# Conv module's end in a conv/retention trunk: output weights' low halves behind the sums, idle full-width products, gate product first, rsqrt as one GpSimd power, smaller first loads

## The chip, the cores and the metric

The kernel runs on one core of a Trainium2 chip. The core has five engines that run side by side, each through its own list of instructions in order: TensorE (PE) for matrix products, VectorE (DVE) and ScalarE (ACT) for element-wise work, GpSimd (POOL) for slower element-wise work, and SyncE (SP), which only issues transfers (ACT issues some too). A semaphore wait holds back everything behind it on that engine. The metric is the device time of one execution in microseconds (us), as the median of several runs; one further execution is taken with a profiler, and all timelines here are from that one.

## The reference

One sequence of 512 tokens, 1024 channels, two layers in float32. Each layer is a mixer and a causal feed-forward block (FFN), each behind an RMS norm and added to the residual stream; at the end stands another RMS norm.

```python
def conv_module(x, w_in, dw_w, dw_b, ln_g, ln_b, w_out):     # mixer of layer 0
    h = x @ w_in                                             # 1024 -> 2048
    a, gate = jnp.split(h, 2, axis=-1)
    h = a * jax.nn.sigmoid(gate)
    h = causal_dwconv(h, dw_w, dw_b)                         # 31 taps per channel
    mu, var = mean(h), mean((h - mu)**2)                     # over the channels
    h = (h - mu) * rsqrt(var + EPS) * ln_g + ln_b
    return silu(h) @ w_out                                   # 1024 -> 1024

def conv_ffn(x, w_in, dw_w, dw_b, w_out):                    # both layers
    a, u = jnp.split(x @ w_in, 2, axis=-1)                   # 1024 -> 2 x 2816
    return (silu(causal_dwconv(a, dw_w, dw_b)) * u) @ w_out  # 3 taps

for i in range(2):
    x = x + mixer_i(rmsnorm(x))          # conv_module, then retention with 4 heads
    x = x + conv_ffn(rmsnorm(x))
return rmsnorm(x)
```

## The kernel before

Channels lie on the 128 partitions (eight groups of 128), tokens along the free axis, so a tile of one channel group is 128x512. Every product of float32 operands is made as three products of halves: each operand is split into a high half, a rounded copy made by ACT, and a low half, the rest, made by DVE. `mm3` (L237 to L239) and `mm3_all` (L244 to L248) issue high x high, low x high, high x low. Weights come in chunks of 1 MB into three buffers `wr`; ACT makes `wh` (L213) and DVE `wl` (L217). A chunk's buffer is free again when both have read it.

A scheduler with a timeline of its own orders each engine's instructions; `issue_after` adds a constraint to that order. The order inside the conv module is written out as a string of words (L44): `m` is the products of one channel group, a and gate, `t` its convolution by taps on ACT, POOL and DVE, `b` and `p` its convolution as products with a banded matrix on TensorE (groups 3, 4, 6, 7), `s` a common shift, `c` the centring of a group's result (L565) with its square (L575), `q` the column sums, `u` the layer norm's statistics and their broadcast, `v` scale, shift and silu to the operands `z`. The tokens are done in two halves, `a` and `b`. The output product `co` (L244 to L248) starts with half `a` while half `b` gets its statistics.

The steps that the change and the prediction touch are these.

- Ten of a group's 31 taps: ACT scales (L520, L523), POOL adds (`pla`, L524). The other 21 are DVE's (`tp`, L533), and DVE adds the two parts (`cs`, L535). Group 5 is the last to end (at 122.81 us).
- The sums of the layer norm: for groups 0 to 5, the centred values and squares are first added up in `lnad` and `lnaq` (L578, L579; groups 4 and 5 by DVE, others by POOL), and TensorE sums them over the partitions in columns (`lna`, `lnb`, L557). Groups 6 and 7 are summed by themselves. Group 7 comes in halves (`cs7a`, `cs7b` by way of `yb7a`, `cq7a` and so on, L499 to L505, with transfers in between).
- The statistics: small DVE operations on 128x2 (L625 to L628), `rsqrt_small` (L274 to L286, a shift and three Newton steps), two diagonal tiles `lnda` (L636), two broadcast products `lnba` (L638).
- `split_behind` says behind which instructions a chunk's low halves may be issued: chunks 8 and 9, the first of the output weights, have the last gate and the last tap sum (L674).
- In the FFN, `ffn_half` makes for each group of 128 the products `fa`, `fu`, the three taps, silu, and the product `fy` (L715). In the last half of the last FFN it also issues one transposition of the residual (`xq`, L941) per group, for a token-major final norm; behind each set of them stand the transfers `xt` on SP's queue.
- The norms' statistics (`Rstd`, L299 to L313): transposes, a reduction, `rsqrt_small`, a diagonal tile (`n0d` to `n3d`), a broadcast product (`n0b` to `n3b`).

## Time and profile before

| | us |
|---|---|
| median of the runs | 1329.04 |
| the profiled execution | 1330.59 |
| its span, first to last instruction | 1328.8 |
| PE busy | 1306.9 (98%) |
| DVE busy | 750.4 (56%) |
| ACT busy | 491.5 (37%) |
| POOL busy | 351.4 (26%) |
| mean granted TensorE clock | 0.989 |

A row of a timeline gives start, duration, engine, line, operation, the tile written and the tiles read with their shape, the count, and in brackets how long the engine sat idle before it and what ended that. Rows of equal kind that follow one another are joined, so a duration with a count above one is the whole of them. Matrix products are pipelined: the step from one to the next is shorter than the duration of one. The granted clock is the share of full speed that TensorE's throttle lets through.

### The profile page before, as it was taken

How to read it: one execution, taken by the hardware profiler on the slowest of the kernel's cores; microseconds unless marked ns; L12 is line 12 of the kernel's file. 1: busy time of each engine (PE TensorE's matmuls, PEld its weight loads, DVE VectorE, ACT ScalarE, POOL GpSimd, SP SyncE). 2: the span in 40 equal slices, each digit the busy share in tenths (PEclk: the TensorE clock that was granted, in tenths of full speed). 3: DMA queues.
4: the chain of work that ended last, by engine and by line, in shares of the span. 5: the costliest groups of instructions: out<-in, count | busy, mean ns of one | idle time of the engine just before them, and what ended most of it. 6: DMA issues, size and time to landing. Idle time of an engine off the chain costs nothing.

```text
span 1328.8 us, 15111 instructions
## 1 busy us (share of the span) xinstructions
PE 1306.9 (98%) x6004; PEld 1090.8 (82%) x6004; DVE 750.4 (56%) x1059; ACT 491.5 (37%) x647; POOL 351.4 (26%) x293
## 2 busy tenths in 40 slices
PE   9999799999999999999999999999999999999997
PEld 7888788888888888878888888888878888888886
DVE  6998667666335554563565644644766462255544
ACT  5545454434223433423333332332534341133332
POOL 1859131687206110220213203203211110011110
PEclk9999699999999999999999999999999999999999
DMA  7543232131322222322332422422143222223121
GB/s 289 215 155 103 72 104 95 66 125 66 125 95 95 95 79 86 137 96 103 91 116 76 130 97 82 159 72 92 67 139 111 95 97 97 103 84 120 55 79 64
DMA packets 39814, 140.49 MB, mean 106 GB/s; under 512 B 11840, under 2 KB 21824, under 8 KB 25536
## 3 DMA queue, kind: packets, MB, share of 16 engines
q1 hardware_dynamic: 36432, 135.15, 29.0%
q10 hardware_dynamic: 3312, 4.38, 1.0%
q8 instruction: 47, 0.77, 0.2%
q14 instruction: 23, 0.19, 0.0%
HBM read 130.07 MB, written 2.10 MB: 99 GB/s over the span
## 4 chain that ended last, share of the span: by engine, by line
PE 91%; DVE 4%; DMA 2%; POOL 1%; ACT 1%; issue 1%; SPq 0%; DVEq 0%; ACTq 0%
PE fu L238 6%; PE fu L237 6%; PE fu L239 6%; PE fa L238 6%; PE fa L237 6%; PE fa L239 6%; PE vg L237 4%; PE vg L238 4%; PE vg L239 4%; PE lo L238 3%; PE lo L239 3%; PE lo L237 3%; PE fo L237 3%; PE fo L238 3%; PE fo L239 3%; PE qk L237 2%
## 5 line engine op out<-in xcount | busy, mean ns | idle before, releaser
L217 DVE TENSOR_TENSOR wl<-wr,wh 128x1024 fp32r<-128x1024 f32 (+1 forms) x222 | 285.7, 1290 | 277.6 <-ACT wh L213 273.5
L213 ACT CAST wh<-wr 128x1024 fp32r<-128x1024 f32 (+1 forms) x222 | 231.4, 1045 | 409.4 <-PE fo L239 82.7
L706 POOL MEMSET ap<- 128x2 f32 x44 | 4.2, 99 | 398.6 <-DVE ft L711 338.6
L715 DVE TENSOR_TENSOR fy<-fu,ft 128x512 f32<-128x512 f32 x44 | 30.3, 689 | 66.6 <-PE fu L239 35.0
L840 POOL TENSOR_TENSOR gg<-gg,gn 128x512 f32<-128x512 f32 x16 | 23.9, 1495 | 153.1 <-ACT gg L839 153.1
L709 ACT ACTIVATE ft<-ap,prm 128x512 f32<-128x512 f32 x44 | 35.7, 814 | 69.4 <-DVE ap L707 69.4
L533 DVE SCALAR_TENSOR_TENSOR tp<-hp,prm,tp 128x512 f32<-128x512 f32 x80 | 55.5, 741 | 0.4
L524 POOL TENSOR_TENSOR pla<-pla,plt 128x512 f32<-128x512 f32 x36 | 49.9, 1387 | 8.3 <-ACT pla L520 4.9
L813 POOL TENSOR_TENSOR rs<-rs 128x512 f32<-128x512 f32 x16 | 26.7, 1687 | 85.8 <-DVE rs L812 81.5
L710 DVE SCALAR_TENSOR_TENSOR ft<-ap,prm,ft 128x512 f32<-128x512 f32 x44 | 35.8, 815 | 17.3 <-ACT ft L709 17.2
L712 ACT ACTIVATE ft<-ft 128x512 f32<-128x512 f32 x44 | 27.9, 633 | 44.8 <-DVE ft L711 44.3
L713 POOL TENSOR_TENSOR ft<-ft,n3r 128x512 f32<-128x512 f32 x22 | 32.3, 1467 | 29.0 <-ACT ft L712 29.0
L713 POOL TENSOR_TENSOR ft<-ft,n1r 128x512 f32<-128x512 f32 x22 | 31.6, 1435 | 28.3 <-ACT ft L712 28.3
L711 DVE SCALAR_TENSOR_TENSOR ft<-ap,prm,ft 128x512 f32<-128x512 f32 x44 | 37.1, 843 | 1.4
L397 DVE TENSOR_TENSOR xT<-ro,xT 128x512 f32<-128x512 f32 x32 | 22.0, 687 | 24.2 <-PE ro L239 24.1
L491 PE MATMUL cph<-ph,cmat 128*128 128x128 f32 x288 | 32.9, 275 | 1.2 <-DMA ph<-hq 1.2
L491 PEld LDWEIGHTS cph<-ph,cmat 128*128 128x128 f32 x288 | 32.7, 192 | 1.7 <-issue 1.4
L523 ACT ACTIVATE plt<-hp,prm 128x512 f32<-128x512 f32 x36 | 25.7, 722 | 18.3 <-POOL pla L524 18.1
L885 POOL TENSOR_TENSOR gg<-gg,on 128x512 f32<-128x512 f32 x16 | 20.2, 1295 | 33.5 <-ACT on L884 33.5
L707 DVE TENSOR_TENSOR ap<-fa,n3r 128x512 f32<-128x512 f32 x22 | 15.1, 691 | 24.6 <-PE fa L239 24.6
L707 DVE TENSOR_TENSOR ap<-fa,n1r 128x512 f32<-128x512 f32 x22 | 15.1, 690 | 17.0 <-PE fa L239 16.9
L751 POOL TENSOR_SCALAR near<-prod 128x512 f32<-128x512 f32 x11 | 23.5, 2136 | 0.9
(1563 smaller groups left out, 3841.0 us busy)
## 6 DMA issues: line engine op xcount, KB each, us to landing
wr<-in_weights_dram SPq DMA_DIRECT2D x107, 1024.0 KB, 4.8
cmat<-in_mats_dram SPq DMA_DIRECT2D x4, 2304.0 KB, 10.5
wr<-in_weights_dram SPq DMA_DIRECT2D x6, 512.0 KB, 3.8
yt<-yq SPq DMA_DIRECT2D x48, 64.0 KB, 2.1
xT<-in_xt_dram SPq DMA_DIRECT2D x4, 512.0 KB, 7.4
xt<-xq SPq DMA_DIRECT2D x32, 48.0 KB, 3.5
ph<-hq SPq DMA_DIRECT2D x16, 64.0 KB, 2.2
dm<-in_decay_dram ACTq DMA_DIRECT2D x4, 256.0 KB, 2.7
```

Of the source, the lines that this page charges most:

```text
L213: latest[0] = act.copy(hi[:, o:o + n], raw[:, s + o:s + o + n])
L217: latest[1] = dve.tensor_tensor(out=lo[:, o:o + n], in0=raw[:, s + o:s + o + n], in1=hi[:, o:o + n].bitcast(F32), op=ALU.subtract)
L237: pe.matmul(ps, wh, xh, start=first, stop=False)
L238: pe.matmul(ps, wl, xh, start=False, stop=False)
L239: pe.matmul(ps, wh, xl, start=False, stop=last)
L491: pe.matmul(ps[:, g * P:(g + 1) * P], mats[i][g][:, s, :], ph[:, g, NSH - 1 - s:NSH - 1 - s + P], start=s == 0, stop=s == NSH - 1)
L524: pool.tensor_tensor(out=pl, in0=pl, in1=tm, op=ALU.add)
L533: dve.scalar_tensor_tensor(out=a, in0=hp[:, t:t + S], scalar=tap(t, i), in1=a, op0=ALU.mult, op1=ALU.add)
L709: act.activation(t, ap[:, 2:], AF.Identity, scale=wc(2), bias=wc(3))
L710: dve.scalar_tensor_tensor(out=t, in0=ap[:, 1:1 + S], scalar=wc(1), in1=t, op0=ALU.mult, op1=ALU.add)
L711: dve.scalar_tensor_tensor(out=t, in0=ap[:, 0:S], scalar=wc(0), in1=t, op0=ALU.mult, op1=ALU.add)
L713: scaled = pool.tensor_tensor(out=t, in0=t, in1=norm.rb, op=ALU.mult)
```

## The change

- *Low halves.* Chunk 8's low halves wait for the last addition to `lnaq` on DVE, chunk 9's for the second `lnda` of the first token half.
- *Idle products.* A new word `w` issues products 128x128 by 128x512 whose result nobody reads: six ahead of the column sums, eight ahead of the first half's broadcast (behind the word `c7a`, ahead of `ua`), six behind it.
- *Gate first.* For groups 2 to 7 the gate product comes ahead of the other, and its weights are loaded first.
- *Statistics of the first norm.* Their transposes are issued after two of the eight steps of group 1's gate product, not ahead of it.
- *Rsqrt.* One GpSimd operation, power with exponents -0.5 from a constant tile, in place of nine or eleven DVE operations. All twelve uses change.
- *First loads.* The input comes as 1, 1, 2, 2, 2 channel groups, the first weights in quarters, two of these on ACT's queue; the identity and the large table of parameters move from ACT's queue to SP's, behind chunk 1; a dummy activation moves behind the first issues.
- *Transpositions* in the last FFN half are issued behind `fy` too.
- A padding tile is 48 columns wide, 16 before.

```diff
-SEQ = ("m0 m1 m2 b3 b4 t0 m3 t1 m4 t2 m5 p3 b6 m6 t5 p4 b7 s c0 c1 m7 c2 c3 p6 c4 c5 p7 q c6 c7a ua")
+SEQ = ("m0 m1 m2 b3 b4 t0 m3 t1 m4 t2 m5 p3 b6 m6 t5 p4 b7 s c0 c1 m7 c2 c3 p6 c4 c5 p7 w6 q c6 c7a w8 ua w6")
...
     for c in range(1, 4):
+        cols("conv_w_in", 0, 0, 8, (D + 256 * c, 256))
         cols("conv_w_in", 0, 0, 8, (256 * c, 256))
-        cols("conv_w_in", 0, 0, 8, (D + 256 * c, 256))
...
     def rsqrt_small(v, n, name):
...
-        dve.tensor_scalar(out=t, in0=v.bitcast(I32), scalar1=1, scalar2=None, op0=ALU.logical_shift_right)
-        dve.tensor_scalar(out=y.bitcast(I32), in0=t, scalar1=-1.0, scalar2=float(0x5F3759DF), op0=ALU.mult, op1=ALU.add)
...
-        for _ in range(3):
-            dve.scalar_tensor_tensor(out=c, in0=y, scalar=-0.5, in1=y, op0=ALU.mult, op1=ALU.mult)
-            dve.tensor_tensor(out=c, in0=c, in1=v, op=ALU.mult)
-            dve.scalar_tensor_tensor(out=y, in0=c, scalar=1.5, in1=y, op0=ALU.add, op1=ALU.mult)
+        pool.tensor_tensor(out=y, in0=v, in1=minus_half[:, :n], op=ALU.pow)
         return y
...
-        early = load_weights(0, 2)
-        for k in range(0, KD, 2):
-            nc.sync.dma_start(xs_all[:, k:k + 2, :], xt_d[:, k:k + 2, :])
-            if k % 4 == 0:
-                next(early)
-        nc.scalar.dma_start(ident, ident_d)
+        early = load_weights(0, 4, (0, 1))
+        for k, n in ((0, 1), (1, 1), (2, 2), (4, 2), (6, 2)):
+            nc.sync.dma_start(xs_all[:, k:k + n, :], xt_d[:, k:k + n, :])
+            if k != 1:
+                next(early)
+        act.activation(ss0, ones[:, 0:1], AF.Sigmoid)
         next(load_weights(1))
-        nc.scalar.dma_start(prm[:, N_FIRST:], cols_d[:, N_FIRST:])
+        nc.sync.dma_start(ident, ident_d)
+        nc.sync.dma_start(prm[:, N_FIRST:], cols_d[:, N_FIRST:])
...
-                eng.tensor_tensor(out=part["q"], in0=part["q"], in1=sq, op=ALU.add)
+                added = eng.tensor_tensor(out=part["q"], in0=part["q"], in1=sq, op=ALU.add)
+                if i in ADD_DVE:
+                    split_behind[N_CONV - 4] = added.ins,
...
-                n0.stats()
-                pg = conv_mm(i, half, "g", w, P)
+                pg = conv_mm(i, half, "g", w, P, n0.stats)
...
-                pa, pg = (conv_mm(i, half, which, wts[which], i % 2 * P) for which in "ag")
+                pg, pa = (conv_mm(i, half, which, wts[which], i % 2 * P) for which in "ga")
...
+        def step_w(n, _):
+
+            ps = psum(f"warm{len(warm)}")
+            warm.append(ps)
+            h = x0[KD - 1][0]
+            for _ in range(n):
+                pe.matmul(ps, h[:, :P], h, start=True, stop=True)
...
         run(SEQ)
-        split_behind[N_CONV - 4] = split_behind[N_CONV - 3] = gate[1], taps_end[0]
+        split_behind[N_CONV - 3] = chain[1],
...
-            dve.tensor_tensor(out=y, in0=pu, in1=t, op=ALU.mult)
+            product = dve.tensor_tensor(out=y, in0=pu, in1=t, op=ALU.mult)
...
-                with tc.issue_after(scaled.ins):
+                with tc.issue_after(scaled.ins), tc.issue_after(product.ins):
                     next(side, None)
```

The orders that come of it, at three places. On POOL, at the end of the taps, before; `pla` with the last number is the last tap group's partial sum, `cs_...` are the results of single groups, numbered by the program:

```order
L524 TENSOR_TENSOR pla_914<-pla_914,plt_8_937 128x512
L469 TENSOR_TENSOR cgr_1082<-cgr_1082,n0r 128x512
L565 TENSOR_TENSOR cs_745<-cs_745,shift 128x512
L565 TENSOR_TENSOR cs_841<-cs_841,shift 128x512
L524 TENSOR_TENSOR pla_914<-pla_914,plt_9_940 128x512
L578 TENSOR_TENSOR lnad<-lnad,cs_745 128x512
L579 TENSOR_TENSOR lnaq<-lnaq,lnsq_1092 128x512
L565 TENSOR_TENSOR cs_965<-cs_965,shift 128x512
L565 TENSOR_TENSOR cs_1004<-cs_1004,shift 128x512
L578 TENSOR_TENSOR lnad<-lnad,cs_841 128x512
L579 TENSOR_TENSOR lnaq<-lnaq,lnsq_1097 128x512
```

and now:

```order
L559 TENSOR_TENSOR cs_834<-cs_834,shift 128x512
L518 TENSOR_TENSOR pla_907<-pla_907,plt_7_927 128x512
L572 TENSOR_TENSOR lnad<-lnad,cs_738 128x512
L573 TENSOR_TENSOR lnaq<-lnaq,lnsq_1085 128x512
L518 TENSOR_TENSOR pla_907<-pla_907,plt_8_930 128x512
L572 TENSOR_TENSOR lnad<-lnad,cs_834 128x512
L573 TENSOR_TENSOR lnaq<-lnaq,lnsq_1090 128x512
L518 TENSOR_TENSOR pla_907<-pla_907,plt_9_933 128x512
L559 TENSOR_TENSOR cs_958<-cs_958,shift 128x512
L559 TENSOR_TENSOR cs_997<-cs_997,shift 128x512
```

`lnad` and `lnaq` of two groups moved from behind the last `pla` to ahead of it.

On DVE, right behind the last tap sum, before; `wl_...` are the low halves of chunks 8 and 9, `cs_1194` is group 7 in its first half of tokens:

```order
L217 TENSOR_TENSOR wl_0_1276<-wr_1273,wh_0_1275 128x1024
L217 TENSOR_TENSOR wl_1024_1280<-wr_1273,wh_1024_1279 128x1024
L217 TENSOR_TENSOR wl_0_1286<-wr_1283,wh_0_1285 128x1024
L217 TENSOR_TENSOR wl_1024_1290<-wr_1283,wh_1024_1289 128x1024
L565 TENSOR_TENSOR cs_1138<-cs_1138,shift 128x512
L578 TENSOR_TENSOR lnad<-lnad,cs_1004 128x512
L578 TENSOR_TENSOR lnad<-lnad,cs_965 128x512
L579 TENSOR_TENSOR lnaq<-lnaq,lnsq_1148 128x512
L579 TENSOR_TENSOR lnaq<-lnaq,lnsq_1153 128x512
L565 TENSOR_TENSOR cs_1194<-cs_1194,shift 128x256
L625 TENSOR_SCALAR lnsta<-lna 128x2
L626 TENSOR_TENSOR lnmsqa<-lnsta 128x2
```

and now, from the last tap sum's successors on:

```order
L573 TENSOR_TENSOR lnaq<-lnaq,lnsq_1146 128x512
L219 TENSOR_TENSOR wl_0_1280<-wr_1277,wh_0_1279 128x1024
L219 TENSOR_TENSOR wl_1024_1284<-wr_1277,wh_1024_1283 128x1024
L559 TENSOR_TENSOR cs_1187<-cs_1187,shift 128x256
L620 TENSOR_SCALAR lnsta<-lna 128x2
L621 TENSOR_TENSOR lnmsqa<-lnsta 128x2
L622 TENSOR_SCALAR lnmsqa<-lnmsqa 128x2
L623 SCALAR_TENSOR_TENSOR lnsta<-lna,lnmsqa 128x2
L631 TENSOR_TENSOR lnda_1257<-ident,lnay 128x256
L629 TENSOR_TENSOR lnsta<-lnsta,lnay 128x2
L631 TENSOR_TENSOR lnda_1261<-ident,lnsta 128x256
L219 TENSOR_TENSOR wl_0_1290<-wr_1287,wh_0_1289 128x1024
```

The four low halves moved from ahead of the sums to behind them, two ahead of the statistics and two behind `lnda`; the last of these four, and the second half of group 7, stand right behind the rows shown.

On DVE in the last FFN, from the norm's statistics on, before:

```order
L285 TENSOR_TENSOR n3c<-n3c,n3v 128x4
L286 SCALAR_TENSOR_TENSOR n3y<-n3c,n3y 128x4
L941 STREAM_TRANSPOSE xq_7818<-xT 128x4x4x32
L308 TENSOR_TENSOR n3d<-ident,n3y 128x512
L217 TENSOR_TENSOR wl_0_7263<-wr_7260,wh_0_7262 128x1024
L941 STREAM_TRANSPOSE xq_7818<-xT 128x4x4x32 x2
L217 TENSOR_TENSOR wl_1024_7267<-wr_7260,wh_1024_7266 128x1024
L707 TENSOR_TENSOR ap_0_7398<-fa_0_7270,n3r 128x512
```

and now:

```order
L291 TENSOR_REDUCE n3v<-n3s 128x4
L292 TENSOR_SCALAR n3v<-n3v 128x4
L298 TENSOR_TENSOR n3d<-ident,n3y 128x512
L219 TENSOR_TENSOR wl_0_7183<-wr_7180,wh_0_7182 128x1024
L219 TENSOR_TENSOR wl_1024_7187<-wr_7180,wh_1024_7186 128x1024
L710 TENSOR_TENSOR ap_0_7306<-fa_0_7190,n3r 128x512
```

The transpositions `xq` that stood ahead of `n3d` and behind it are gone from here, and with them the steps of rsqrt.

More of the change, by code (lines that the diff above doesn't have):

```diff
@@ L152, in trunk @@
     conv_scope = ExitStack()
-    sp.tile([P, LINE // 16], F32, tag="pad", bufs=1, name="pad")
+    sp.tile([P, 3 * LINE // 16], F32, tag="pad", bufs=1, name="pad")
     cv = conv_scope.enter_context(tc.tile_pool(name="cv", reuse_waits="tile", bufs=2))
@@ L179, in trunk, with load_weights @@
     latest = [None, None, None]
-    def load_weights(i, parts=1):
+    def load_weights(i, parts=1, on_act=()):
         nk, ncol = descs[i]
@@ L187, in load_weights @@
             with tc.issue_after(behind[i]) if i in behind else nullcontext():
-                latest[2] = nc.sync.dma_start(raw[:, j * n:(j + 1) * n], weights_d[i, :, j * n:(j + 1) * n])
+                latest[2] = (nc.scalar if j in on_act else nc.sync).dma_start(raw[:, j * n:(j + 1) * n],
+                                                                              weights_d[i, :, j * n:(j + 1) * n])
             yield
@@ L253, in trunk @@
     keep_warm(N_WARM)
+    minus_half = cp.tile([P, NTB], F32, name="minus_half")
+    pool.memset(minus_half, -0.5)
     ident = cp.tile([P, P], F32, name="ident")
@@ L269, in rsqrt_small @@
     def rsqrt_small(v, n, name):
-        t = sp.tile([P, 8], I32, tag="rq_i", name=name + "i")[:, :n]
         y = sp.tile([P, 8], F32, tag="rq_y", name=name + "y")[:, :n]
-        c = sp.tile([P, 8], F32, tag="rq_c", name=name + "c")[:, :n]
-        dve.tensor_scalar(out=t, in0=v.bitcast(I32), scalar1=1, scalar2=None, op0=ALU.logical_shift_right)
-        dve.tensor_scalar(out=y.bitcast(I32), in0=t, scalar1=-1.0, scalar2=float(0x5F3759DF), op0=ALU.mult, op1=ALU.add)
-        if n == 1:
-            w = sp.tile([P, 8], F32, tag="rq_w", name=name + "w")[:, :1]
-            dve.tensor_scalar(out=w, in0=v, scalar1=-0.5, scalar2=None, op0=ALU.mult)
-            for _ in range(3):
-                dve.scalar_tensor_tensor(out=c, in0=y, scalar=w, in1=y, op0=ALU.mult, op1=ALU.mult)
-                dve.scalar_tensor_tensor(out=y, in0=c, scalar=1.5, in1=y, op0=ALU.add, op1=ALU.mult)
-            return y
-        for _ in range(3):
-            dve.scalar_tensor_tensor(out=c, in0=y, scalar=-0.5, in1=y, op0=ALU.mult, op1=ALU.mult)
-            dve.tensor_tensor(out=c, in0=c, in1=v, op=ALU.mult)
-            dve.scalar_tensor_tensor(out=y, in0=c, scalar=1.5, in1=y, op0=ALU.add, op1=ALU.mult)
+        pool.tensor_tensor(out=y, in0=v, in1=minus_half[:, :n], op=ALU.pow)
         return y
@@ L419, in trunk @@
                 next(halves)
-            n0.split(k)
+                part_hi = latest[0].ins
+            with tc.issue_after(part_hi) if k == 1 else nullcontext():
+                n0.split(k)
         x0 = n0.xs
@@ L443, in trunk, with conv_mm @@
         cs, hps, pls = {}, {}, {}
-        def conv_mm(i, half, which, w, o):
+        def conv_mm(i, half, which, w, o, inside=None):
             t0, t1 = HALF[half]
@@ L448, in conv_mm @@
             for k in range(KD):
+                if inside and k == 2:
+                    inside()
                 xh, xl = x0[k]
@@ L602, in step_m @@
                 if i % 2 == 0 and half != "b":
-                    for which in "ag":
+                    for which in "ga":
                         wts[which] = weights(ahead=min(2, KD - 1 - state["used"]))
-                pa, pg = (conv_mm(i, half, which, wts[which], i % 2 * P) for which in "ag")
+                pg, pa = (conv_mm(i, half, which, wts[which], i % 2 * P) for which in "ga")
             waiting.append((conv_phases_in if i in ON_PE else conv_glu, (i, half, pg, pa)))
```

2 lines of the change are left out of this document (1 added, 1 removed).

## The prediction

> **What bounds the kernel now.** I read the waits of TensorE first, then the granted clock by stretches of 10 us, then the timelines of the engines around the places these name. TensorE is busy 98% of the span, so only its waits and its clock can be won. Its three longest waits, and a short one in the last FFN (the last figure is the longest single one, us):
>
> ```profile
> PE lnba L638 <- DVE lnda L636: 3.5, 1, 3.5
> PE lna L557 <- DVE lnad L578: 3.1, 1, 3.1
> PE n3b L311 <- DVE n3d L308: 1.8, 1, 1.8
> ...
> PE fu L238 <- DVE wl L217: 0.4, 1, 0.4
> ```
>
> The first two lie at the end of the conv module, the third in the statistics before the last FFN. The stretches (ten us each; busy time of PE, PE's weight loads, DVE, ACT, POOL, then TensorE's granted clock, DMA share, GB/s) show the same places at a reduced clock, and DVE without a gap before them:
>
> ```profile
> 90.00:100.00 10.00, 10.00 (x71) 9.22 (x71) 10.00 (x17) 5.58 (x8) 9.00 (x7) 1.00 0.37 127
> ...
> 130.00:140.00 10.00, 6.85 (x45) 6.69 (x44) 7.47 (x7) 3.51 (x7) 4.51 (x3) 0.79 0.24 37
> ...
> 970.00:980.00 10.00, 8.20 (x28) 5.64 (x27) 6.89 (x14) 2.69 (x3) 0.00 (x0) 0.83 0.15 34
> ```
>
> What the sums wait for at the conv module's end, on POOL and then DVE, by start, duration, line:
>
> ```profile
> 102.21 1.27 POOL L524 TENSOR_TENSOR pla<-pla,plt 128x512 f32<-128x512 f32 x1 [2.76 <-ACT pla L520]
> ...
> 122.81 0.69 DVE L535 TENSOR_TENSOR cs<-tp,pla 128x512 f32<-128x512 f32 x1 [2.62 <-POOL pla L524]
> 123.41 8.30 DVE L217 TENSOR_TENSOR wl<-wr,wh 128x1024 fp32r<-128x1024 f32 x4
> ...
> 133.31 2.48 DVE L578 TENSOR_TENSOR lnad<-lnad,cs 128x512 f32<-128x512 f32 x2
> 135.71 1.48 DVE L579 TENSOR_TENSOR lnaq<-lnaq,lnsq 128x512 f32<-128x512 f32 x2
> ...
> 135.94 0.98 PE L557 MATMUL lna<-ones,lnad 128*128 128x1 f32 x4 [3.15 <-DVE lnad L578]
> ```
>
> Four low halves (L217) stand between the last tap sum and the layer-norm sums, and TensorE starts the sums as lnad ends. The rest up to the output product, with the transfers of the last channel group:
>
> ```profile
> 134.54 0.63 ACT L575 ACTIVATE lnsq<-cs 128x512 f32<-128x512 f32 x1 [0.49 <-POOL lnaq L579]
> ...
> 135.33 0.38 ACT L499 COPY yb7b<-cph 128x256 f32<-128x256 f32 x1
> 138.08 1.15 SPq L188 DMA_DIRECT2D wr<-in_weights_dram  x2
> 146.06 0.73 ACT L505 ACTIVATE cs<-cq7b,prm 128x256 f32<-128x256 f32 x1 [6.00 <-DMA cq7b<-yb7b]
> 147.59 0.42 DVE L636 TENSOR_TENSOR lnda<-ident,lnay 128x256 f32<-128x256 f32 x1
> 150.18 0.37 ACT L648 COPY lnmba<-lnba 128x256 f32<-128x256 f32 x1 [1.87 <-PE lnba L638]
> 150.58 0.42 DVE L653 TENSOR_TENSOR cs<-lnba,cs 128x256 f32<-128x256 f32 x1 [1.63 <-ACT lnmba L648]
> 152.59 1.22 PE L244 MATMUL co<-z0h,wh 128*128 128x256 f32 x4 [0.66 <-ACT z0h L660]
> ```
>
> ACT's wait for cq7b is long because two weight loads (SP, 138.08) are in flight beside it; but lnmba waited for lnba, so the statistics, not cq7b, ended last.
>
> **The start.** Rsqrt, from its first to the operation that uses it:
>
> ```profile
> 27.94 0.17 DVE L274 TENSOR_SCALAR n0i<-n0v 128x4 int32<-128x4 int32 x1
> 30.12 0.69 DVE L308 TENSOR_TENSOR n0d<-ident,n0y 128x512 f32<-128x512 f32 x1
> ```
>
> 2.18 us go; one GpSimd power comes. No row shows a power; the nearest are
>
> ```profile
> L706 POOL MEMSET ap<- 128x2 f32 x44 | 4.2, 99 | 398.6 <-DVE ft L711 338.6
> L751 POOL TENSOR_SCALAR near<-prod 128x512 f32<-128x512 f32 x11 | 23.5, 2136 | 0.9
> ```
>
> 0.10 us for a tiny operation and 2.14 for the dearest full one. With 2 to 4 elements to a partition it is nearer to the small one; I take 0.5, plus 0.1 for handing over. So the gate product's evacuation, from which DVE works on without a gap, comes 1.6 us earlier (0 to 2.1). Smaller first loads and the statistics' transposes moved behind two steps of product advance TensorE, and cost nothing else: all of that work lies ahead of the conv end, which DVE and POOL set, and it counts only as that cover. Gate first swaps two equal products and two loads: 0.
>
> **The conv module's end.** By the orders shown with the change, one pair of low halves (chunk 8) now follows the sums, the other (chunk 9) follows lnda. But POOL has more to do before the last tap sum: lnad and lnaq of two more channel groups moved ahead of it, 20 operations in place of 16, each at
>
> ```profile
> L524 POOL TENSOR_TENSOR pla<-pla,plt 128x512 f32<-128x512 f32 x10 | 12.9, 1287 | 3.2 <-ACT pla L520 2.8
> ...
> 30.73 1.22 DVE L217 TENSOR_TENSOR wl<-wr,wh 128x1024 fp32r<-128x1024 f32 x1
> ```
>
> (the second row is a low half while POOL is free). Step by step: chain start 102.21 - 1.6 = 100.6; 20 x 1.287 = 25.7, to 126.3; the tap sum 0.7, to 127.0; two centrings on POOL, 2.6, to 129.6; four additions on DVE at 0.74 (1.48 / 2), to 132.6; TensorE's sums start near 131.8, 4 us earlier. Two low halves, 2.4, to 135.0; centring 0.4, its square on ACT 0.4 and the last four column sums 1.0, to 136.8; four small operations 0.8, power 0.6, to 138.2; lnda twice, 1.0, to 139.2; two low halves, 2.4, to 141.6; centring 0.4, to 142.0, where L653 can start. From L653 to the first co took 2.0 (150.58 to 152.59): 144.0.
>
> Two things may end later. Eight idle products stand before lnba: at half clock they take 8 x 0.45 = 3.6 (0.22 at full clock, by the steps quoted below), to 140.4, then lnba 2.1 and six more, up to 2.7, and two groups for the other half, 0.85: 146.0, and about 144.8 if the clock is back for the six. And cq7b: 10.7 us passed from yb7b to it. yb7b moves to about 131 (it stood on ACT behind the square at 134.54, which waited for lnaq), so unchanged it lands at 141.7, and with the 2.25 us from there to lnmba that ACT worked, co starts at 146.4. It should land sooner, since the loads need buffers that the moved low halves free: chunk 11's at 135.0, after cq7b's pieces are issued, chunk 12's only at 141.6. The next weights are wanted after co's first half of the columns, 48 groups of 0.48 or 23 us, which covers their delay. I take 145.0: a gain of 7.6 (5 to 9).
>
> TensorE's price for co's groups of four, by the chain of waits, and the low half of z1:
>
> ```profile
> 154.66 0.85 PE co L248 x4
> 157.37 0.48 PE co L244 x4
> 155.39 0.41 DVE L661 TENSOR_TENSOR z1l<-cs,z1h 128x256 fp32r<-128x256 f32 x1
> ```
>
> From 152.59 to 156.36 (154.66 and two groups) four groups took 3.77 and not 4 x 0.48 = 1.92: 1.85 lost. At full clock co would want z1l 2.4 us after its start, and DVE delivers 3.2 after; so 1.0 can be won. Idle products of 3 to 6 us make that likely, not sure: I take 0.5 (0 to 1.0).
>
> **The last FFN.** Here the rows are
>
> ```profile
> 968.77 0.17 DVE L302 TENSOR_SCALAR n3v<-n3v 128x4 f32<-128x4 f32 x1
> ...
> 972.89 0.39 PE L238 MATMUL fa<-n3x7h,wl 128*128 128x512 f32 x1
> 973.11 0.39 PE L239 MATMUL fa<-n3x7l,wh 128*128 128x512 f32 x1
> 973.97 0.71 DVE L941 STREAM_TRANSPOSE xq<-xT 128x512 f32<-128x512 f32 x1 [2.84 <-DMA xt<-xq]
> 974.60 0.65 DVE L308 TENSOR_TENSOR n3d<-ident,n3y 128x512 f32<-128x512 f32 x1
> 975.30 1.87 PE L311 MATMUL n3b<-n3d,ones 128*128 128x512 f32 x2 [1.80 <-DVE n3d L308]
> 979.05 0.39 PE L239 MATMUL fu<-n3x1l,wh 128*128 128x512 f32 x1
> ```
>
> and, for the same broadcast at full clock in the first FFN,
>
> ```profile
> L311 PE MATMUL n1b<-n1d,ones x2: 590/590/591, 217.3 to 217.7; 128*128 128x512 f32 x2
> ```
>
> A transpose that waits for a DMA stands ahead of n3d. By the new order the transposes are gone from there, behind the FFN's products. n3d follows the power at once, and TensorE needs it 3.7 us after n3v (968.94; 973.33 less 0.65). From 973.33 (973.11 and one step of 0.22) to 979.05, 5.7 us, TensorE did two n3b (0.9 at full clock, by n1b's two starts 0.4 apart) and five products (1.1): 3.7 lost. The wait for a low half, 0.4, which stood behind three more transposes, goes with them: 4.1 (3.0 to 4.5). The transposes' DMAs now share SP's queue later with the weight loads; a wait of a load there has the stock of three buffers to hide behind.
>
> The clock fell here after a wait of 1.8 us. TensorE: Matmul & The Clock Gate in the Trainium skill (Why this matters for your kernels) asks only that gaps stay below about 3 us; by that rule it should have held, so the trace disagrees. By the rule, which makes nothing of column sums one wide, the conv end would stay at full clock after the change and the sum below would be 1.5 better (rival 2).
>
> **The tail.**
>
> ```profile
> 1322.56 0.15 DVE L274 TENSOR_SCALAR fr3i<-fv 128x1 int32<-128x1 int32 x1
> 1324.08 0.16 DVE L281 SCALAR_TENSOR_TENSOR fr3y<-fr3c,fr3y 128x1 f32<-128x1 f32 x1
> ```
>
> Nothing lies beside this: 1.7 goes, 0.6 comes, 1.1 gained (-0.5 to 1.5). The other rsqrts (n1, n2, the retention's) are not waited for by TensorE: 0.
>
> **Sum:** 7.6 + 0.5 + 4.1 + 1.1 = 13.3 us. The profiled execution took 1330.6 (span 1328.8 and 1.8 around it), so 1317.3; the median of the runs is 1.55 below it, so 1316.
>
> **Rivals.** (1) *The conv end gives little*: POOL's four operations (5.1 us) and the chunk-8 halves ahead of the last centring become the new wait, slowed as the four were before (8.30 against 4 x 1.22), and cq7b lands as late as before. Then first co near 148 to 150, gain 2.6 to 4.6 there and nothing in the clock: 1319 to 1321. (2) *The clock holds*: co and the idle products run at full speed, co starts at 144.0: 1.5 more, 1314. Against it stands n3b's drop; and the column sums after the first six idle products last over 4 us, which for the clock were idle before: they ran from 135.94 on, and the groups at 154.66 still had the half clock's price. (3) *Slower: the power is dear.* No row bounds the length of a power. Each us beyond 0.5 is paid at the start, at lnda and in the tail: three for one; n3d has room for 3.6, then it pays too. 13.3 = 3 (p - 0.5) + (p - 3.6): from p = 4.6 us each the kernel is slower; at 6 us, 13.3 - 16.5 - 2.4 = -5.6, 1335. Nothing in the trace excludes it. If only the first call is slow, its excess is paid once, at the start. The GPSIMD Engine Reference in the Trainium skill (2.1, Instruction dispatch) gives about 6 us for the first call of a newly loaded kernel, which no run here shows; by that the estimate would be 1321. (4) *It does not do what it says*: the idle products push lnba back as far as the sums came forward; the n3 and tail gains stay: 1324.
>
> **Numbers.** Forecast 0.62, (1) 0.16, (2) 0.08, (3) 0.09, (4) 0.05. The range reaches to (1) and (2) with the ends of the power's price (0.1: 1.2 better, 2.1: 4.8 worse): 1310 to 1325, with about 2 in 10 outside. A difference of 2%, 26.6 us, is about what a measurement of this kernel tells from none. Faster by that needs 1302.5, more than all waits and clock losses above together: 0.01. Slower by it needs a power of some 11 us: 0.03.
>
> **What would show it.** Right: lna starting by 132.5 with low halves behind lnaq; first co by 145; n3b without a wait and 970 to 980 at full clock; power rows on POOL below 1 us. Wrong: power rows of several us; lnba or cq7b ending after 145; a weight wait in the last FFN.

## The result and the profile after

The changed kernel takes 1320.49 us (median of 4 runs, 1320.17 to 1320.65) against 1328.88 of the kernel before in the same session: a ratio of 0.9937, interval 0.9918 to 0.9957. That is 8.4 us less, well under the 2% that decide between faster and same. One of the four runs of the kernel before took 2011.7 us; without it their median is 1328.71, and the gain 8.2 us. The forecast was 1316, in a range of 1310 to 1325. Its profiled execution took 1320.42 with a span of 1318.3 at a mean clock of 0.995; that of the kernel before had 1330.59, 1328.8 and 0.989.

TensorE's waits in the kernel after (waiting operation, what ended the wait; total, times, longest, us):

```profile
PE ca L246 <- ACT wh L215: 2.1, 1, 2.1
PE lna L551 <- DVE cs L559: 1.5, 1, 1.5
...
PE lna L551 <- DVE lnad L572: 0.7, 1, 0.7
PE co L246 <- ACT z0h L655: 0.7, 1, 0.7
PE co L250 <- DVE z1l L656: 0.6, 2, 0.4
```

The waits of 3.5, 3.1 and 1.8 us are gone: lnba and n3b don't stand in the list, and the first column sums wait 0.7. At the top now stands the wait of the very first product for its weights, 2.1 us, which was 0.9 before; second is a wait of the column sums for the last channel group (1.5).

The granted clock in the stretches named in the prediction (columns as there):

```profile
130.00:140.00 10.00, 7.71 (x58) 7.05 (x57) 5.95 (x8) 3.46 (x7) 1.82 (x2) 0.87 0.36 94
140.00:150.00 10.00, 9.27 (x45) 8.10 (x46) 7.65 (x21) 5.64 (x11) 1.10 (x2) 0.79 0.40 136
150.00:160.00 10.00, 9.57 (x77) 9.26 (x76) 6.75 (x18) 5.23 (x12) 4.68 (x6) 1.00 0.03 11
...
970.00:980.00 10.00, 10.00 (x45) 8.27 (x45) 8.99 (x11) 5.33 (x7) 3.04 (x4) 1.00 0.49 162
```

The clock still falls at the conv end, from 137.39 to 144.22 by the trace's clock records (before: 135.87 to 156.35), but it is back before co begins. At 970 to 980 it stays full.

The conv end after, by engine (start, duration, line, operation, and in brackets the idle time before it and what ended it). DVE:

```profile
128.10 0.69 DVE L529 TENSOR_TENSOR cs<-tp,pla 128x512 f32<-128x512 f32 x1 [9.38 <-POOL pla L518]
...
133.74 0.68 DVE L573 TENSOR_TENSOR lnaq<-lnaq,lnsq 128x512 f32<-128x512 f32 x1
134.34 2.35 DVE L219 TENSOR_TENSOR wl<-wr,wh 128x1024 fp32r<-128x1024 f32 x2
138.86 0.43 DVE L559 TENSOR_TENSOR cs<-cs,shift 128x256 f32<-128x256 f32 x1 [2.17 <-ACT cs L499]
...
142.83 0.43 DVE L631 TENSOR_TENSOR lnda<-ident,lnay 128x256 f32<-128x256 f32 x1 [0.83 <-POOL lnay L276]
...
143.77 2.35 DVE L219 TENSOR_TENSOR wl<-wr,wh 128x1024 fp32r<-128x1024 f32 x2
146.04 0.42 DVE L559 TENSOR_TENSOR cs<-cs,shift 128x256 f32<-128x256 f32 x1
146.37 0.42 DVE L648 TENSOR_TENSOR cs<-lnba,cs 128x256 f32<-128x256 f32 x1
```

ACT, and then TensorE, of the same stretch:

```profile
133.17 0.38 ACT L493 COPY yb7b<-cph 128x256 f32<-128x256 f32 x1
...
138.10 0.73 ACT L499 ACTIVATE cs<-cq7a,prm 128x256 f32<-128x256 f32 x1 [4.55 <-DMA cq7a<-yb7a]
...
145.51 0.37 ACT L643 COPY lnmba<-lnba 128x256 f32<-128x256 f32 x1 [0.91 <-PE lnba L633]
```

```profile
133.96 0.58 PE L551 MATMUL lna<-ones,lnad 128*128 128x1 f32 x4 [0.75 <-DVE lnad L572]
...
141.07 3.54 PE L664 MATMUL warm<-n0x7h 128*128 128x512 f32 x8
144.44 1.03 PE L633 MATMUL lnba<-lnda,ones 128*128 128x256 f32 x4
...
148.37 0.74 PE L246 MATMUL co<-z0h,wh 128*128 128x256 f32 x4 [0.73 <-ACT z0h L655]
```

The first output product starts at 148.37 instead of 152.59. The order is as planned: a pair of low halves (L219) behind lnaq, the other behind lnda, each at 2.35 us. DVE then stands idle for 2.2 us until ACT has evacuated the first transfer of the last channel group, cq7a.

In the last FFN and at the rsqrts (timelines and tile views after):

```profile
963.02 0.17 DVE L292 TENSOR_SCALAR n3v<-n3v 128x4 f32<-128x4 f32 x1
964.32 0.69 DVE L298 TENSOR_TENSOR n3d<-ident,n3y 128x512 f32<-128x512 f32 x1 [1.13 <-POOL n3y L276]
...
967.59 1.02 PE L301 MATMUL n3b<-n3d,ones 128*128 128x512 f32 x2
```

```profile
L276 POOL TENSOR_TENSOR n0y<-n0v,minus_half x1: 1027/1027/1027, 28.6 to 28.6; 128x4 f32<-128x4 f32 x1
L276 POOL TENSOR_TENSOR n1y<-n1v,minus_half x1: 1017/1017/1017, 207.8 to 207.8; 128x4 f32<-128x4 f32 x1
L276 POOL TENSOR_TENSOR lnay<-lnsta,minus_half x1: 715/715/715, 142.1 to 142.1; 128x2 f32<-128x2 f32 x1
L276 POOL TENSOR_TENSOR fr3y<-fv,minus_half x1: 543/543/543, 1313.2 to 1313.2; 128x1 f32<-128x1 f32 x1
```

n3d now follows the power at once, 3.3 us ahead of n3b. The program runs fourteen powers (the list of changes says twelve): one takes some 0.54, 0.72 to 0.88 or 1.03 us with 1, 2 or 4 elements to a partition.

Set end to end, the two profiled executions differ by 4.2 us at the first co, 5.2 at the first product of the first FFN (200.47 and 195.31), 5.7 at n3's sum (n3s, 967.41 and 961.66), 9.4 at the start of the last FFN's output products (`lo`, 1092.15 and 1082.73) and 10.5 at the end. The medians differ by 8.4 only; why is the subject of one experiment below.

### The profile page after: what moved, and what is told of

Read it like the earlier page. It is cut to its first block, busy times and chain, and to the rows that moved or that the text cites. A ratio compares the mean times of both kernels' runs of the same rounds, so it can differ in the third digit from the quotient of the medians.

```text
span 1318.3 us, 15033 instructions
## 1 busy us (share of the span) xinstructions
PE 1304.4 (99%) x6024; PEld 1088.6 (83%) x6024; DVE 724.2 (55%) x913; ACT 490.4 (37%) x647; POOL 357.8 (27%) x308
## 4 chain that ended last, share of the span: by engine, by line
PE 88%; POOL 5%; DVE 3%; issue 1%; ACT 1%; DMA 1%; ACTq 0%; POOLq 0%; DVEq 0%
PE fu L241 6%; PE fa L241 6%; PE fa L239 6%; PE fu L239 6%; PE fa L240 6%; PE fu L240 6%; PE vg L241 4%; PE vg L239 4%; PE vg L240 4%; POOL pla L518 3%; PE lo L241 3%; PE fo L240 3%; PE fo L241 3%; PE lo L239 3%; PE lo L240 3%; PE fo L239 3%
## 5 line engine op out<-in xcount | busy, mean ns | idle before, releaser
L219 DVE TENSOR_TENSOR wl<-wr,wh 128x1024 fp32r<-128x1024 f32 (+1 forms) x222 | 281.5, 1270 | 284.8 <-ACT wh L215 280.8
L341 POOL TENSOR_TENSOR n2acc<-n2acc,n2sq 128x512 f32<-128x512 f32 x6 | 9.1, 1511 | 48.7 <-ACT n2sq L340 48.5
## 6 DMA issues: line engine op xcount, KB each, us to landing
cmat<-in_mats_dram SPq DMA_DIRECT2D x4, 2304.0 KB, 10.2
```

What stands on the lines that cost most here:

```text
L219: latest[1] = dve.tensor_tensor(out=lo[:, o:o + n], in0=raw[:, s + o:s + o + n], in1=hi[:, o:o + n].bitcast(F32), op=ALU.subtract)
```

## The experiments

Theory after the result: the sum's mechanisms are all there; the conv end won less because the work ahead of it came late and a transfer took long, and the two profiled executions differ by more than two ordinary ones. Rivals: the conv end is held by the idle products or the gate's order; the power or the first loads cost something that the sum put at nothing; one part of the change carries all of it.

**The first loads.** The change's kernel with the first loads as before:

```diff
-        early = load_weights(0, 4, (0, 1))
-        for k, n in ((0, 1), (1, 1), (2, 2), (4, 2), (6, 2)):
-            nc.sync.dma_start(xs_all[:, k:k + n, :], xt_d[:, k:k + n, :])
-            if k != 1:
-                next(early)
         act.activation(ss0, ones[:, 0:1], AF.Sigmoid)
+        early = load_weights(0, 2)
+        for k in range(0, KD, 2):
+            nc.sync.dma_start(xs_all[:, k:k + 2, :], xt_d[:, k:k + 2, :])
+            if k % 4 == 0:
+                next(early)
+        nc.scalar.dma_start(ident, ident_d)
...
```

> The changed kernel with the first loads of before (input in four transfers of two channel groups, first weights in halves, identity and parameters on ACT's queue). Theory: the new loads delay the first product (7.54 us, at half clock, in place of 7.27) and with it the first hp (36.68 in place of 36.07); that delay runs through DVE and POOL to the end of the conv module. So here: first product at 7.3, first hp 0.6 to 1.2 us earlier, first co 0.6 to 1.2 us earlier than 148.4, time 1319.3 to 1319.9. Rival (the transfers of cq7a and cq7b, or POOL, set the end, whatever the start): first co within 0.2 of 148.4, 1320.5. Rival 2 (the new loads do help): 1321 to 1322.

Measured: 1319.32 (1318.43 to 1321.67), ratio 0.9929, interval 0.9914 to 0.9944. TensorE's first product in the kernel after, and in this one:

```profile
7.54 0.69 PE L246 MATMUL ca<-n0x0h,wh 128*128 128x512 f32 x1 [2.06 <-ACT wh L215]
8.03 0.63 PE L246 MATMUL cg<-n0x0h,wh 128*128 128x512 f32 x1
```

```profile
7.53 0.50 PE L246 MATMUL ca<-n0x0h,wh 128*128 128x512 f32 x1 [1.19 <-ACT wh L215]
7.87 0.39 PE L246 MATMUL cg<-n0x0h,wh 128*128 128x512 f32 x1
```

The smaller loads bring the first product no earlier, and TensorE's clock is at 0.5 from 7.68 to 11.10 in the kernel after: products of 0.63 us instead of 0.39. The product of `a` and gate, `hp`, where DVE's chain begins, with the new loads and with the old:

```profile
36.68 0.69 DVE L467 TENSOR_TENSOR hp<-ca,cgr 128x512 f32<-128x512 f32 x1 [1.48 <-POOL cgr L463]
```

```profile
35.40 0.69 DVE L465 TENSOR_TENSOR hp<-ca,cgr 128x512 f32<-128x512 f32 x1 [1.48 <-POOL cgr L461]
...
145.69 0.74 PE L246 MATMUL co<-z0h,wh 128*128 128x256 f32 x4 [0.28 <-ACT z0h L653]
```

So the new loads cost 1.3 us there in this pair; the 1.2 of the medians lies within the runs' spread. Not every execution has the drop at the start: of the seven profiles with the new loads and twelve warm-up products, four have it. In one of the others, the run with the gate second below, `hp` starts at 35.96, 0.6 later than with the old loads. The first output product comes 2.7 us earlier with the old loads, more than was expected of them: cq7a also takes 3.1 us here in place of 4.9, of which more below.

**The gate's order.** As before, gate second:

```diff
-                    for which in "ga":
+                    for which in "ag":
```

with the two loads swapped back.

> The changed kernel with the products of groups 2 to 7 and their weight loads in the order of before, gate second. The scheduler then puts lnad and lnaq of one more group behind the last pla on POOL (18 operations ahead of it, not 20). Theory (what POOL does ahead of the last tap sum sets the sums' start): the last tap sum 2.6 us earlier, but two additions follow it, and the sums start within 1 us of 133.96; 1319.5 to 1321. Rival (gate first brings POOL's gate multiplication forward and is what made room): sums later by 2 us or more, 1322 to 1323. Rival 2 (the order costs all of its 5 us): 1318.

Measured: 1319.9 (1318.78 to 1320.21), ratio 0.9928, interval 0.9911 to 0.9945: no difference that the runs resolve. The last tap sum starts at 122.59 instead of 128.10, but DVE then waits 5.8 us until ACT's evacuation, and lnad starts at 130.39, 1.5 earlier. TensorE's sums start where they did, at once behind its own products:

```profile
129.12 1.35 DVE L559 TENSOR_TENSOR cs<-cs,shift 128x512 f32<-128x512 f32 x1 [5.83 <-ACT cs L499]
...
133.98 0.50 PE L551 MATMUL lna<-ones,lnad 128*128 128x1 f32 x4
```

First co 147.88. In the kernel after, lnad does wait for POOL (1.17 us, behind the late tap sum); with POOL 5.5 us earlier, the evacuation and TensorE's own products end last instead, at nearly the same time. So the order of POOL's work is worth 1.5 us to lnad and nothing to the sums.

**The low halves.** Back ahead of the sums:

```diff
-                if i in ADD_DVE:
-                    split_behind[N_CONV - 4] = added.ins,
...
-        split_behind[N_CONV - 3] = chain[1],
+        split_behind[N_CONV - 4] = split_behind[N_CONV - 3] = gate[1], taps_end[0]
```

> The changed kernel with all four low halves behind the last gate and tap sum again, ahead of the sums. Theory (the low halves' place is worth what they take, 4.9 us alone and 8.3 beside POOL, less the two that then no longer stand between lnda and the first scaled half, 2.4): first co 2.5 to 5 us later than 148.4, 1323 to 1325.5. Rival (cq7a, which landed at 138.1, sets the statistics, so the place of the low halves is free): 1320 to 1321.

Measured: 1326.29 (1324.98 to 1328.27), ratio 0.998, interval 0.9971 to 0.999. This is the largest single part of the conv end: 5.8 us of medians, somewhat above what was expected, and the first co comes 5.7 us later. DVE and TensorE in its timeline:

```profile
128.78 6.79 DVE L219 TENSOR_TENSOR wl<-wr,wh 128x1024 fp32r<-128x1024 f32 x4
...
138.13 0.98 PE L551 MATMUL lna<-ones,lnad 128*128 128x1 f32 x4 [4.88 <-DVE lnad L572]
...
154.08 0.74 PE L246 MATMUL co<-z0h,wh 128*128 128x256 f32 x4 [0.28 <-ACT z0h L653]
```

The four halves take 6.79 us in a row, the sums wait 4.9 us and then run at half clock (0.98 us for a group, against 0.58 in the kernel after).

**The idle products.** Left out:

```diff
-SEQ = ("m0 m1 m2 b3 b4 t0 m3 t1 m4 t2 m5 p3 b6 m6 t5 p4 b7 s c0 c1 m7 c2 c3 p6 c4 c5 p7 w6 q c6 c7a w8 ua w6")
+SEQ = ("m0 m1 m2 b3 b4 t0 m3 t1 m4 t2 m5 p3 b6 m6 t5 p4 b7 s c0 c1 m7 c2 c3 p6 c4 c5 p7 q c6 c7a ua")
```

> The changed kernel without the twenty idle products. Theory (they bring the clock back before co): lnba starts 1 us earlier but runs at half clock, co's first groups of four cost 0.85 in place of 0.48, first co within 1 us of 148.4, lnbb 0.5 to 1.5 us later than 157.8: 1320.5 to 1322. Rival (they only stand in the way, the eight ahead of lnba above all): 1319 to 1319.8, and granted clock in 140 to 150 the same or better.

Measured: 1322.59 (1321.37 to 1323.87), ratio 0.9951, interval 0.9936 to 0.9966: 2.1 us more, above the expected range. The four runs lie in two pairs, near 1321.4 and near 1323.8, and the profiled one is of the upper pair. TensorE, with the column sums at half clock and lnba, and the clock by stretches:

```profile
134.45 0.90 PE L551 MATMUL lna<-ones,lnad 128*128 128x1 f32 x4 [2.10 <-DVE lnad L572]
...
145.13 2.08 PE L633 MATMUL lnba<-lnda,ones 128*128 128x256 f32 x4 [2.10 <-DVE lnda L631]
```

```profile
140.00:150.00 10.00, 6.77 (x27) 5.78 (x26) 5.96 (x16) 4.29 (x8) 0.72 (x1) 0.50 0.30 102
150.00:160.00 10.00, 10.00 (x65) 9.92 (x66) 7.94 (x22) 6.71 (x15) 5.04 (x6) 0.75 0.21 88
```

lnba starts 0.7 later than with them, where 1 us earlier was expected; but cq7a's evacuation is 0.8 later in this execution, so the idle products neither advance the statistics nor visibly hold them up. They buy the clock of what follows. The clock records show 0.5 from 134.55 to 155.03, over ten groups of column sums back to back; lnba takes 2.08 us and not 1.03, co starts 1.8 later, and the second broadcast comes at 161.05 instead of 157.80.

**The power.** The rsqrt on DVE again, as before:

```diff
-        pool.tensor_tensor(out=y, in0=v, in1=minus_half[:, :n], op=ALU.pow)
+        dve.tensor_scalar(out=t, in0=v.bitcast(I32), scalar1=1, scalar2=None, op0=ALU.logical_shift_right)
+        dve.tensor_scalar(out=y.bitcast(I32), in0=t, scalar1=-1.0, scalar2=float(0x5F3759DF), op0=ALU.mult, op1=ALU.add)
...
```

> The changed kernel with rsqrt on DVE as before in all twelve places. Theory (the power takes 1.0 us with 4 elements a row, 0.7 with 2, 0.54 with 1, and 0.13 to hand over each way; the DVE steps took 2.18, 2.17 and 1.7 to 2.0): start 0.9 later, through DVE to the sums; lnda 1.2 later, of which the idle products ahead of lnba hide part, but the low halves behind lnda not; tail 1.1 later: 1322.5 to 1323.7. Rival (only the tail counts, the rest is hidden): 1321.5.

Measured: 1354.37 (1351.84 to 1355.24), ratio 1.0181, interval 1.0166 to 1.0196: 34 us more, far beyond what either theory gave. It lies in no wait: the products themselves are slower, everywhere. The change has an edit that the prediction did not price, a padding tile of 48 columns instead of 16, and taking out the power brings back three small tiles. So two more kernels, with the padding as before:

```diff
-    sp.tile([P, 3 * LINE // 16], F32, tag="pad", bufs=1, name="pad")
+    sp.tile([P, LINE // 16], F32, tag="pad", bufs=1, name="pad")
```

alone,

> The changed kernel with the padding tile of 16 columns, as before, and nothing else. It shifts all tiles behind it by 128 bytes. Theory (in the run with rsqrt on DVE the three tiles of rsqrt came back, 384 bytes, while the padding stayed at 48 columns; its products were 2.5% slower everywhere, 34 us, since operands then lay 128 bytes off): 1352 to 1356 here too, with products of the FFN 0.233 us apart in place of 0.227. Rival (the slow run came from the DVE steps or the order): 1320.5.

and together with the old rsqrt.

> The changed kernel with rsqrt on DVE and the padding tile of 16 columns, so that all tiles lie as in the kernel before. Theory (the power's price): what was expected of the run with rsqrt on DVE, 1322.5 to 1323.7: start 0.9 later, lnda 1.2 later of which a part shows, tail 1.1 later. Rival (only the tail counts): 1321.5. Rival 2 (the slowness of that run was not the padding): 1354.

Measured: 1352.21 (1351.76 to 1352.66), ratio 1.0172, interval 1.0154 to 1.0191, for the padding alone; 1323.95 (1323.48 to 1324.42), ratio 0.996, interval 0.9946 to 0.9973, for both. The same 100 us of the first FFN in the kernel after, and with the old padding (PE first, its count of products in brackets):

```profile
220.00:320.00 100.00, 100.00 (x442) 82.78 (x442) 65.09 (x70) 37.33 (x47) 71.70 (x55) 1.00 0.27 95
```

```profile
220.00:320.00 100.00, 100.00 (x431) 80.43 (x430) 65.28 (x69) 37.21 (x48) 68.62 (x54) 1.00 0.28 100
```

TensorE is busy throughout and its clock is full in both, but 431 products stand where 442 stood: 0.232 us for one instead of 0.226, 2.5%. The four kernels make a square:

| | rsqrt on DVE | power on GpSimd |
|---|---|---|
| padding 16 columns | 1323.95, 443 products | 1352.21, 431 products |
| padding 48 columns | 1354.37, 432 products | 1320.49, 442 products |

Each of the two edits alone slows the products; both together, or neither, leave them fast. The 32 columns move every tile allocated behind the padding by 128 bytes to a partition, and the old rsqrt's three tiles move them too: by their sizes (four buffers of 32 bytes each) by 384 bytes. The two fast layouts are then 256 bytes apart and the slow ones 128 bytes off them, which would fit a period of 256 bytes; that is argued from four layouts only, and which tiles must lie where was not tried. So the padding edit gains nothing of its own, but without it the kernel after takes 31.7 us more, and the power would have cost 28.3 us (1352.21 against 1323.95). With a fast layout on both sides, the power is worth 1323.95 - 1320.49 = 3.5 us.

**The transposes.** The kernel before with the one edit in the last FFN:

```diff
-                with tc.issue_after(scaled.ins):
+                with tc.issue_after(scaled.ins), tc.issue_after(product.ins):
```

> The kernel before with the transposes of the last FFN half behind fy, nothing else. Theory: no wait of n3b, full clock from 970 to 980, no wait for the low half before it: 4.0 us of the whole gain, 1324.8 (1324.3 to 1325.3). Rival (the transposes' transfers then hold up weight loads or the last sums): a new wait of PE in the last FFN, gain under 2.5, 1326.5 or more.

Measured: 1326.41 (1326.04 to 1327.04), ratio 0.9978, interval 0.9968 to 0.9988: 2.9 us by the medians of the session (1329.27), not 4.0, though n3b's wait is gone whole. So the kernel before was profiled a second time, unchanged.

> The kernel before, unchanged, once more with a profile. Question: the profiled execution of before took 1330.59 us, 1.8 more than the median of its other runs, and the transposes alone gave 2.6 and not the 4.1 us that its trace shows. Theory (whether the 1.8 us wait at n3b makes the clock fall depends on where the clock's windows of 3.413 us lie in an execution): here n3b waits 1.8 us as before, and if the run takes about 1329 the granted clock from 970 to 980 is whole, if about 1331 it is 0.83. Rival (the two executions differ elsewhere): same clock at n3, other stages differ by 1.5 us or more.

Measured: 1328.05, span 1326.2. TensorE and the clock at the same place:

```profile
974.37 1.13 PE L311 MATMUL n3b<-n3d,ones 128*128 128x512 f32 x2 [1.68 <-DVE n3d L308]
```

```profile
970.00:980.00 10.00, 8.32 (x35) 6.21 (x35) 6.84 (x11) 4.40 (x6) 0.00 (x0) 1.00 0.24 44
```

n3b waits here too, but the clock holds: n3b's two products start 0.5 apart, not 0.8. The drop behind a wait of 1.80 us in the first profile did not follow a wait of 1.68 us in this one. From n3s to the first `lo` this execution takes 1.7 us less than the first profile; another 0.8 lies ahead of n3s; at the conv end the clock's drop lasted 17.07 us here and not 20.48. Of the kernel before's other 34 runs in the three sessions of experiments, 29 lie between 1328.1 and 1329.8 and five between 1330.7 and 1331.5. The five may be executions with the drop at n3b, but none of the 34 has a profile, and their mean clock (0.988 to 0.989, that of the 29 0.989 to 0.992) does not tell them apart.

**The start's clock.** The change with twice the idle products at the start:

```diff
-N_WARM = 12
+N_WARM = 24
```

> The changed kernel with 24 warm-up products of 128x128 at the start and not 12; they lie in the wait for the first weights. Theory 1 (the new first loads let TensorE idle long enough for the clock to fall in the first window): clock whole from the first product on, n0s at least 1 us earlier relative to the first product, first hp 0.5 to 1.2 us earlier than 36.68. Theory 2 (a 16 KB fetch of instructions, seen at 135.5 among the pieces of cq7a, delays that by 1.5 us): the fetch shifts against yb7a with the number of TensorE instructions, and cq7a takes 3.0 to 3.1 us from yb7b where the fetch lies after its pieces, 4 to 5 where it lies among them. Time 1318.5 to 1320 if either holds. Rival (neither: the start is set by transfers, cq7a by the weight load): 1320.5, cq7a 4.9 from yb7b.

Measured: 1319.42 (1318.9 to 1320.16), ratio 0.9922, interval 0.9907 to 0.9936. The clock is full from the first product on, but the first weights landed later in this execution and the product starts at 8.89; `hp` at 37.05 is no earlier. The start's dropped clock is thus not the whole price of the new loads; their late arrival is the other part. cq7a is evacuated 3.1 us after yb7b's copy here, against 4.9 in the kernel after. The DMA view of that stretch (135.4 to 138.2) in the kernel after, GB/s in 40 slices and the instruction queue:

```profile
GB/s 95 55 315 161 96 55 48 95 172 92 62 77 150 136 48 40 102 158 99 55 7 7 11 11 7 7 11 11 11 7 11 0 0 702 234 0 0 0 468 468
...
q8 instruction: 1, 0.02, 2.5%
```

Between yb7b's copy and cq7a's evacuation this queue carries one packet of 0.02 MB, and behind it the transfer's pieces trickle at 7 to 11 GB/s. The next weight load is not what slows them: by the trace's transfer records its first piece starts at 137.72, behind the last small one (137.56). Over all profiles: of the seven that have such a packet there, six took 4.2 to 5.3 us (the kernel after, the two with old padding, and those with the gate second, without idle products or without the power) and one 3.06 (the old loads, where the packet starts only 0.3 us ahead of the evacuation); the seven that have none took 3.04 to 3.14. That the packet is the cause is thus likely, not shown: no run removed it alone.

**A better version.** The change with the old loads, the column sums of group 6 first, the idle products split into 2, 3, 4, 8 and 6, and the first half of the last chunk's low halves behind the last centring:

```diff
-SEQ = ("m0 m1 m2 b3 b4 t0 m3 t1 m4 t2 m5 p3 b6 m6 t5 p4 b7 s c0 c1 m7 c2 c3 p6 c4 c5 p7 w6 q c6 c7a w8 ua w6")
+SEQ = ("m0 m1 m2 b3 b4 t0 m3 t1 m4 t2 m5 p3 b6 m6 t5 p4 b7 s c0 c1 m7 c2 c3 p6 c4 c5 p7 w2 c6 w3 q w4 c7a w8 ua w6")
...
-                    for ins in split_behind.get(i, ()):
+                    for ins in split_behind.get((i, s), split_behind.get(i, ())):
...
-                (dve if i in CEN_DVE else pool).tensor_tensor(out=c, in0=c, in1=sh, op=ALU.subtract)
+                centred = (dve if i in CEN_DVE else pool).tensor_tensor(out=c, in0=c, in1=sh, op=ALU.subtract)
+            if half == "a":
+                split_behind[N_CONV - 3, 0] = centred.ins,
```

> The changed kernel with the first loads of before; the column sums of group 6 ahead of those of groups 0 to 5; idle products as 2 before, 3 and 4 among the column sums, 8 and 6 as in the change; chunk 9's first pair of low halves behind the centring of cs7a, its second behind lnda. Theory (the clock falls during the narrow column sums, and DVE's two low halves behind lnda and the eight products at half clock end together): clock whole through the sums, the last column sum near 137, lnba near 139.5, first co 143 to 144 against 145.7 with the old loads alone: 1316.5 to 1317.5. Rival (narrow products and short waits still let the clock fall): idle products at half clock push the last sum back, first co 145 to 146.5, 1318.5 to 1320.

Measured: 1317.71 (1315.51 to 1318.23), ratio 0.9904, interval 0.9887 to 0.992: the fastest of all, 2.8 us below the change by medians, though the intervals overlap at their ends (0.9918 to 0.992). The first co was expected at 143 to 144 and stands at 145.56. TensorE:

```profile
137.64 3.76 PE L664 MATMUL warm<-n0x7h 128*128 128x512 f32 x8
141.20 1.91 PE L633 MATMUL lnba<-lnda,ones 128*128 128x256 f32 x4
...
145.56 0.73 PE L246 MATMUL co<-z0h,wh 128*128 128x256 f32 x4
```

Although no gap of over 0.1 us is left in TensorE from 130.4 to 137.6, the clock falls at 136.77, and the eight idle products run at half clock to 141.2, while lnda was there at 140.4. One of the four runs, the one of 1315.51 us, has a mean clock of 0.999: that leaves some 1 to 4 us of half clock in the whole execution, less than the 6.83 us of this drop, so there the clock seems to have held at the conv end. It has no profile. With four of them in place of eight:

```diff
-SEQ = ("m0 m1 m2 b3 b4 t0 m3 t1 m4 t2 m5 p3 b6 m6 t5 p4 b7 s c0 c1 m7 c2 c3 p6 c4 c5 p7 w2 c6 w3 q w4 c7a w8 ua w6")
+SEQ = ("m0 m1 m2 b3 b4 t0 m3 t1 m4 t2 m5 p3 b6 m6 t5 p4 b7 s c0 c1 m7 c2 c3 p6 c4 c5 p7 w2 c6 w3 q w4 c7a w4 ua w6")
```

> The last version with four idle products ahead of lnba and not eight. Theory (at half clock the eight ran until 141.2, while lnda was there at 139.4 to 139.8, and lnmba then held DVE for 1.65): lnba starts within 0.3 of lnda, the first scaled half (L648) at 142 to 142.8, first co 1 us earlier, 1316 to 1317. Rival (the clock then comes back one window of 3.4 us later, and co starts at half clock): within 0.5 of 1317.7.

```profile
138.19 2.05 PE L664 MATMUL warm<-n0x7h 128*128 128x512 f32 x4
140.43 2.08 PE L633 MATMUL lnba<-lnda,ones 128*128 128x256 f32 x4 [0.18 <-DVE lnda L631]
```

Measured: 1318.68 (1317.16 to 1319.04), ratio 0.9918, interval 0.9905 to 0.9932. lnba comes 0.8 us earlier, and the first co at 144.96, yet the time is not below that of eight. Those 0.6 us lie under what these runs resolve.

## Why the prediction was right, and where it was off

The range held the time, and faster or slower by 2% was rightly excluded. The gain was 8.4 us where the sum had 13.3. Of its own signs of being right, n3b's came, but lna started at 133.96 and not by 132.5, the first co at 148.37 and not by 145, the powers on four elements took just over 1 us, and lnba ended after 145 (145.5), which it had named a sign of being wrong. The mechanisms were right and sizes were off; the time itself is that of rival 1. Step by step:

- **The conv end, 7.6, is the term that was mis-sized: 4.2.** The chain's start was put 1.6 us earlier (100.6); it came 0.7 later (102.95). Two steps failed there. "I take 0.5, plus 0.1 for handing over": the power took 1.03, and with handing over 1.1. And the smaller first loads, which were to "cost nothing else", cost 1.3 at `hp` in this pair (0.6 in an execution without the start's drop): they were taken to lie under the cover of DVE and POOL, but `hp` is where DVE's chain starts. Together that is 1.8 of the 2.35 by which the chain started late; the rest was not traced. The 20 operations took 25.1 us and the sum had 25.7, so the tap sum was 1.8 late (128.10 for 126.3), and the centrings, additions and sums followed 1.8 to 2.2 late (sums at 133.96 for 131.8).
- **cq7a was left out.** The sum let DVE centre the last group right behind the first pair of low halves, at 135.0. This one waits for cq7a until 138.86. The prediction weighed cq7b, which moved up as argued and ended at 143.1, not last; its twin ahead of it took 4.9 us in place of 3.1. That adds 2.2 us of DVE's idle time. In the run with the old loads, where the loads' cost and cq7a's delay are both gone, the first co stands at 145.69, 0.7 from the forecast: these two carry most of what was missing. At lnda the delay was 4.6 (142.83 for 138.2), and L653's counterpart stood at 146.37 for 142.0.
- **The allowance of 1 us for idle products** was not needed at the end: the eight products ran at half clock as warned (3.4 us) and lnba behind them at full clock, to 145.5, but the second pair of low halves, to 146.1, ended later still. So 4.4 late became 3.4 at the first co. Low halves beside a free POOL took 1.2 us each, as the sum had them.
- **co's clock, 0.5 of 1.0, came whole:** 1.0 more at the first product of the FFN, with z1l waiting 0.4. The drop itself came as in the forecast, not as in rival 2.
- **The last FFN, 4.1, is right for the profiled pair** (5.7 to 9.4 is 3.7, and the fu wait's 0.4 ahead of it is gone) **and too large for the medians.** The second profile of the kernel before is 1.7 us shorter from n3s to `lo`: that part was a dropped clock, which not every execution has. The prediction took the 1.55 us between profile and median for an offset of both kernels; this drop is its likely source. The kernel after has no such offset: 1320.42 profiled, 1320.49 median.
- **The tail, 1.1, came as forecast** (9.4 to 10.5). That the other rsqrts are worth nothing fits the square's 3.5 us: between its two fast profiles with the new loads the first co is 2.3 us apart (150.68 and 148.37), and the tail adds some 1.1.

Against the profiled pair, 13.3 became 10.2: -3.4 at the conv end, +0.5 in co's clock, small ends elsewhere. The missing offset adds 1.5, and 1316 becomes 1320.5.

Of the rivals, (1) has the right numbers, first co near 148 to 150 and 1319 to 1321, but half of its mechanism: a transfer was late, while the low halves were not slowed and the clock did come back. Rival 2 did not happen: the clock fell at the conv end in every profile of this case. In the Trainium skill, TensorE: Matmul & The Clock Gate (Why this matters for your kernels) asks that gaps stay under about 3 us; at n3b 1.68 us agreed with it and 1.80 did not, and at the conv end of the kernel after the clock fell with no gap above 0.75 us in the ten us ahead of it. Rival 3 is refuted by the power rows. The GPSIMD Engine Reference in the Trainium skill (2.1, Instruction dispatch) has some 6 us for a newly loaded kernel's first call; n0y, the first, took 1027 ns and n1y 1017, and n0d waited 1.1 us for the first, so no such price appeared here. Rival 4 is refuted by the pair (the first co came 4.2 us earlier) as well as by the run without idle products.

What was missing was a rival: the padding. With it left at 16 columns, the same edits make the kernel 1.7% slower than before. The prediction gave slower a chance of 0.03 by a dear power only, and never said what the padding line does. The experiments do not add up to the whole either: undoing the low halves costs 5.8, the power 3.5, the idle products 2.1, the loads -1.2, the gate's order -0.6, and the transposes are worth some 2.9, in sum 12.5 where 8.4 was gained. The conv end's parts overlap: a wait that one of them leaves can hide what another wins; which pairs do so was not tried.
